# When the passes over the ada weights are issued among the weight loads of the first phase: a table of due counts in place of one rate per load

## The chip, the cores and the metric

One core of one Trainium2 chip runs the kernel, in float32 throughout. The time is that of one execution on the device, in microseconds (us): the median of three runs. A profiled execution is a run of its own; its span is what the trace covers.

## The reference, cut to what matters

One layer over 256 tokens of width 2048. A vector `c` conditions it: `mod` is a matrix-vector product with a weight of 2048 x 12288, cut into six vectors, and the first two (shift and scale) go into the first activation `h`, which the projections read.

```python
c_act = jax.nn.silu(c)
mod = (c_act @ w_ada[l] + b_ada[l])[:, None, :]
sh1, sc1, g1, sh2, sc2, g2 = jnp.split(mod, 6, axis=-1)
h = rmsnorm(x, ng[0]) * (1.0 + sc1) + sh1
proj = h @ w_in[l]
...
x = x + g1 * rmsnorm(mixed @ w_out[l], ng[1])
h = rmsnorm(x, ng[2]) * (1.0 + sc2) + sh2
f = jnp.square(jax.nn.relu(h @ w_ff1[l])) @ w_ff2[l]
x = x + g2 * rmsnorm(f, ng[3])
```

## The kernel before

**Products.** Every float32 weight is split into a high part and a remainder, and a product takes three matmuls (`natural_block`, L197 to L203): high by high, high activation by low weight, low activation by high weight. So a weight tile costs a cast on ACT (`h_v`, L152), a subtraction on DVE (`l_v`, L153) and three matmuls for each half of the tokens.

**The first phase** (L436 to L460) computes the columns `v_a`, `v_b`, `r_a` of `proj`: 12 result tiles (`nat`) of 512 columns. The 16 slices of `h` (128 features each, `hT`, two to a tile) come in four steps of 2, 4, 5 and 5 (`STEPS`). In a step, each slice's load brings the weights of the first four result tiles for that slice; then twice as many loads bring those of the other eight, which need all slices of the step. A load is one transfer of 1 MB (`r_v`) that feeds 24 matmuls, and there are 48, numbered 0 to 47: the slices 0 and 1 are loads 0 and 1, the slices 2 to 5 are loads 6 to 9, 6 to 10 are loads 18 to 22, 11 to 15 are loads 33 to 37. At the end of a step each result tile is evicted from PSUM: copied by ACT in the first step (`COPY`, L409), added by DVE in the others (`TENSOR_TENSOR`, L411).

**Rows of h.** Slice `k` of `h` needs the shift and the scale for its 128 features. Each is one pass (`ada_step`, L288): a transfer of 1 MB (`ad_0_k` or `ad_1_k`) and one DVE instruction of 2048 columns (L296) that multiplies by `c` and sums. There are 32 passes for the 16 slices, numbered here 1 to 32 in the order `ad_0_0`, `ad_1_0`, `ad_0_1`, and so on; all but the first two go through a pool of two buffers, so a pass's transfer is issued only when the pass two before it is done. `h_tile` (L353) then makes the slice: ACT adds the bias to the shift (L355) after the first pass, forms the scale (L356) after the second, writes the high part (L366) and the full value (L367); DVE multiplies by the norm (L363, for up to four slices at once) and subtracts for the low part (L368).

**Who sets the order.** `chunk` (L415) is called once per load. `ada_until` (L397) issues passes until a count is reached, then the load and its split are issued, then `h_ready` (L402) makes each slice whose passes have been issued. The count is the larger of what the slice at hand needs and of a rate (0.86 a load, L27 and L424). A scheduler places the instructions on each engine's queue, and each queue is executed in the order so made; all these transfers are issued by SP, in its order.

```python
ada_until(min(2 * KT, max(2 * need, 2 + int(ADA_RATE * at))))
```

Of the kernel before, what the change touches and what calls it, by code (L numbers as in the profile page):

```python
# [17 lines left out]
KT = D // P  # L18
# [5 lines left out]
FB = 8  # L24
EPS = 1e-6
NEG = -1.0e30
ADA_RATE = 0.86  # L27
APART = ("ss", "se", "ew")

SLOTS = 24  # L30
STEPS = (2, 4, 5, 5)
QUAD = 4
# [4 lines left out]
def trunk_kernel(ctx, tc, xT, xn, cT, ada, bcol, ngcol, w_alow, w_gup, gg_row,  # L37
# [118 lines left out]
    def wsplit(src, name, n=2048, step=2048):  # L156

        raw = load(src, f"r_{name}", n, step)
        return [split_one(raw, name, u, min(1024, n - 1024 * u)) for u in range((n + 1023) // 1024)]
# [179 lines left out]
    nat = vA + vB + rA  # L339
    with tc.tile_pool(name="st", bufs=1) as st:  # L340
# [53 lines left out]

        ready = [2, 0]

        def ada_until(n):  # L397
            while ready[0] < n:
                made["ada"] = next(steps)
                ready[0] += 1  # L400

        def h_ready():  # L402
            while ready[1] < KT and 2 * (ready[1] + 1) <= ready[0]:
                h_tile(ready[1])
                ready[1] += 1
# [9 lines left out]
        def chunk(need):  # L415
            nonlocal at
            with ExitStack() as order:
                order.enter_context(tc.issue_after(late.ins))
                if at < 2:
                    order.enter_context(tc.high_priority())  # L420
                    h_ready()
                    order.enter_context(tc.issue_after((lows or placed)[-1].ins))
                    order.enter_context(tc.issue_after(made["dve"].ins))
                ada_until(min(2 * KT, max(2 * need, 2 + int(ADA_RATE * at))))  # L424
                if at < 2:
                    h_ready()
            with ExitStack() as order:
                order.enter_context(tc.issue_after(placed[0].ins))
                if at < 2:
                    order.enter_context(tc.issue_after(made["act"].ins if at else late.ins))  # L430
                parts = wsplit(w_nat[at], f"v_{at}", step=2048 if at else 1024)
            h_ready()
            at += 1
            return parts

        for g, size in enumerate(STEPS):  # L436
            pv = [awake if g + n == 0 else pp(f"pv_{g}_{n}") for n in range(QUAD)]
            for k in range(size):
                parts = chunk(k0 + k + 1)
                for n in range(QUAD):  # L440
                    for i in range(NTOK):
                        natural_block(pv[n][:, i], hT[k0 + k], block(parts, n, 512), i, k == 0, k == size - 1)
                    if k == size - 1:
                        evict(nat[n], pv[n], g)
                if g + k == 0:

                    for _ in range(AWAKE):
                        pe.matmul(pv[0][:, 0, 0:384], negm[:, P:2 * P], carry, start=False, stop=False)
            todo = [(n, k) for n in range(QUAD, len(nat)) for k in range(size)]
            for j, (n, k) in enumerate(todo):  # L450
                if j % 4 == 0:
                    parts = chunk(k0 + size)
                if k == 0:
                    pv = pp(f"pv_{g}_{n}")
                for i in range(NTOK):
                    natural_block(pv[:, i], hT[k0 + k], block(parts, j % 4, 512), i, k == 0, k == size - 1)
                if k == size - 1:
                    evict(nat[n], pv, g)
            k0 += size
# [9 lines left out]
    if True:  # L469
# [8 lines left out]
        for u in range(2):  # L478
# [5 lines left out]
            for k in range(8):  # L484
                kt = 8 * u + k
# [573 lines left out]
```

## Time and profile before

| | before |
|---|---|
| median of 3 runs (lowest, highest) | 1798.25 us (1797.36, 1798.36) |
| the profiled execution, its span | 1800.57 us, 1798.6 us |
| PE busy, share of the span | 1772.9 us, 99% |
| DVE busy | 1283.8 us, 71% |
| ACT busy | 889.0 us, 49% |
| HBM | 428.18 MB read, 239 GB/s over the span |

The span lacks what lies around the program on the device, 1.97 us in that execution. An engine's busy time is the union of its instructions; matmuls overlap in the records (each is shown for 0.39 us where they start every 0.23 us), so a PE that is busy is not one that loses nothing. The first phase lies between 23 and 297 us of the span.

### The profile page before, as it was taken

What the parts mean: (1) busy time and instruction counts of PE and PEld (TensorE: products, weight loads), DVE (VectorE), ACT (ScalarE), POOL (GpSimd) and SP (SyncE); (2) the same over time, 40 slices, a digit from 0 to 9 for tenths busy, and PEclk for the clock granted to TensorE, in tenths of its full rate; (3) what the DMA queues carried; (4) which work ended last, traced back from release to release, by engine and by line L of the source; (5) the groups of instructions that cost most, each with busy time, mean ns of one, the idle gap of its engine ahead of it and who ended that gap; (6) DMA issues with size and microseconds to landing.
All of it is one profiled execution on the core that took longest, in us unless ns stands there. A gap on an engine that the chain in (4) does not pass through costs nothing.

```text
span 1798.6 us, 21945 instructions
## 1 busy us (share of the span) xinstructions
PE 1772.9 (99%) x8627; PEld 1471.8 (82%) x8627; DVE 1283.8 (71%) x1486; ACT 889.0 (49%) x1214; POOL 15.9 (1%) x34
## 2 busy tenths in 40 slices
PE   7999999999999999999999999999999999999997
PEld 4787887877888888888888878888888888888886
DVE  7899976887777788887786567565656565656566
ACT  6644444655553455555644455443434343434443
POOL 0000000000000000000000000000000000000000
PEclk9999999999999999999999999999999999999999
DMA  9888865666788776767777653555555555555552
GB/s 352 336 314 331 357 238 194 259 224 234 294 319 300 285 295 251 266 257 269 292 305 271 245 209 141 192 186 201 186 194 188 187 187 189 187 196 185 202 186 98
DMA packets 62313, 431.72 MB, mean 240 GB/s; under 512 B 7345, under 2 KB 7521, under 8 KB 11138
## 3 DMA queue, kind: packets, MB, share of 16 engines
q1 hardware_dynamic: 60000, 425.78, 63.6%
q10 hardware_dynamic: 2210, 4.54, 0.8%
q8 instruction: 67, 1.10, 0.2%
q14 instruction: 36, 0.29, 0.0%
HBM read 428.18 MB, written 2.12 MB: 239 GB/s over the span
## 4 chain that ended last, share of the span: by engine, by line
PE 92%; DVE 4%; issue 1%; ACT 1%; DMA 1%; POOL 0%; SPq 0%; POOLq 0%; DVEq 0%; ACTq 0%
PE pb_f L174 19%; PE pa_f L202 6%; PE pa_f L201 6%; PE pa_f L200 6%; PE pb_kb L174 5%; PE pb_qb L174 5%; PE pv L201 4%; PE pv L200 4%; PE pv L202 4%; PE pb_qa L174 3%; PE pb_ka L174 2%; DVE ad L296 2%; PE pa_yb L200 2%; PE pa_yb L201 2%; PE pa_wo L202 2%; PE pa_wo L200 2%
## 5 line engine op out<-in xcount | busy, mean ns | idle before, releaser
L153 DVE TENSOR_TENSOR l_f<-r_f,h_f 128x1024 fp32r<-128x1024 f32 x248 | 303.7, 1225 | 202.2 <-ACT h_f L152 198.5
L152 ACT CAST h_f<-r_f 128x1024 fp32r<-128x1024 f32 x248 | 261.0, 1053 | 262.9 <-PE pa_f L202 196.4
L174 PE MATMUL pb_f<-h,h_f 128*128 128x512 f32 x960 | 336.1, 399 | 0.0
L174 PE MATMUL pb_f<-h,l_f 128*128 128x256 f32 x960 | 259.8, 281 | 0.0
L296 DVE SCALAR_TENSOR_TENSOR ad<-ad,cb 128x2048 f32<-128x2048 f32 x96 | 219.1, 2286 | 20.0 <-DMA ad<-in_ada_dram 17.2
L174 PEld LDWEIGHTS pb_f<-h,h_f 128*128 128x128 f32 x960 | 177.0, 188 | 39.1
L200 PE MATMUL pa_f<-h_f,ft 128*128 128x512 f32 x512 | 199.3, 389 | 0.0
L202 PE MATMUL pa_f<-h_f,ft 128*128 128x512 f32 x512 | 199.2, 389 | 0.0
L201 PE MATMUL pa_f<-l_f,ft 128*128 128x512 f32 x512 | 199.2, 389 | 0.0
L174 PEld LDWEIGHTS pb_f<-h,l_f 128*128 128x128 f32 x960 | 181.3, 189 | 5.8
L200 PE MATMUL pv<-h_v,hT 128*128 128x512 f32 x384 | 148.6, 394 | 6.8 <-ACT hT L366 3.6
L201 PE MATMUL pv<-l_v,hT 128*128 128x512 f32 x384 | 149.6, 393 | 0.5 <-DVE l_v L153 0.5
L202 PE MATMUL pv<-h_v,hT 128*128 128x512 f32 x384 | 147.7, 389 | 0.0
L153 DVE TENSOR_TENSOR l_v<-r_v,h_v 128x1024 fp32r<-128x1024 f32 x96 | 114.5, 1219 | 31.2 <-ACT h_v L152 31.0
L152 ACT CAST h_v<-r_v 128x1024 fp32r<-128x1024 f32 x96 | 97.8, 1048 | 56.0 <-PE pv L202 48.5
L201 PEld LDWEIGHTS pa_f<-l_f,ft 128*128 128x128 f32 x512 | 96.1, 188 | 20.1
L202 PEld LDWEIGHTS pa_f<-h_f,ft 128*128 128x128 f32 x512 | 96.1, 188 | 19.9
L200 PEld LDWEIGHTS pa_f<-h_f,ft 128*128 128x128 f32 x512 | 96.1, 188 | 19.7
L200 PEld LDWEIGHTS pv<-h_v,hT 128*128 128x128 f32 x384 | 71.7, 188 | 25.8 <-ACT h_v L152 6.6
L174 PE MATMUL pb_qb<-hT,h_qb 128*128 128x512 f32 x256 | 92.1, 400 | 0.0
L174 PE MATMUL pb_kb<-hT,h_kb 128*128 128x512 f32 x256 | 90.7, 393 | 0.0
L201 PEld LDWEIGHTS pv<-l_v,hT 128*128 128x128 f32 x384 | 72.4, 189 | 17.3 <-DVE l_v L153 2.2
(284 smaller groups left out, 3286.5 us busy)
## 6 DMA issues: line engine op xcount, KB each, us to landing
r_f<-in_w_f_dram SPq DMA_DIRECT2D x124, 1024.0 KB, 4.8
ad<-in_ada_dram SPq DMA_DIRECT2D x96, 1024.0 KB, 5.5
r_v<-in_w_nat_dram SPq DMA_DIRECT2D x47, 1024.0 KB, 7.3
r_ga<-in_w_ga_dram SPq DMA_DIRECT2D x16, 1024.0 KB, 4.9
r_ya<-in_w_ao_dram SPq DMA_DIRECT2D x16, 1024.0 KB, 5.7
r_qb<-in_w_qb_dram SPq DMA_DIRECT2D x16, 1024.0 KB, 5.6
r_kb<-in_w_kb_dram SPq DMA_DIRECT2D x16, 1024.0 KB, 4.8
r_gb<-in_w_gb_dram SPq DMA_DIRECT2D x16, 1024.0 KB, 4.9
```

The source lines that it names most:

```text
L152: s_.copy(hi[:, 0:m], raw)
L153: lows.append(v_.tensor_tensor(out=lo[:, 0:m], in0=raw, in1=hi[:, 0:m].bitcast(F32), op=ALU.subtract))
L174: pe.matmul(o, l, r, start=kt == 0 and n == 0, stop=kt == KT - 1 and n == 1)
L200: pe.matmul(ps, ah, w[0], start=start, stop=False)
L201: pe.matmul(ps, ah, w[1], start=False, stop=False)
L202: return pe.matmul(ps, al, w[0], start=False, stop=stop)
L296: return v_.scalar_tensor_tensor(out=raw, in0=raw, scalar=1.0, in1=cb, op0=ALU.mult, op1=ALU.mult, accum_out=mods[:, m, kt:kt + 1])
```

## The change

The rate goes. A table `due` gives, for the loads 2 to 36, how many passes are to have been issued by that load. It is anchored at one load ahead of the last slice of each step but the first (loads 8, 21 and 36, with 12, 22 and 32 passes) and runs evenly from one anchor to the next, starting with 4 passes at load 1. What a slice needs at its own load still holds as a minimum.

```diff
-ADA_RATE = 0.86
...
         ready = [2, 0]
 
+        due, a0, n0, o, kt = {}, 1, 4, 0, 0
+        for size in STEPS:
+            kt += size
+            o += size
+            if o > 2:
+                for a in range(a0 + 1, o - 1):
+                    due[a] = n0 + (2 * kt - n0) * (a - a0) // (o - 2 - a0)
+                a0, n0 = o - 2, 2 * kt
+            o += size * (len(nat) - QUAD) // 4
+
         def ada_until(n):
...
-                ada_until(min(2 * KT, max(2 * need, 2 + int(ADA_RATE * at))))
+                ada_until(min(2 * KT, max(2 * need, due.get(at, 0))))
```

Passes issued by the time a load is issued:

| load | 1 | 2 | 3 | 4 | 5 | 6 | 7 | 8 | 9 | 10 | 12 | 14 | 17 | 20 | 21 | 22 | 24 | 32 | 35 | 36 |
|---|---|---|---|---|---|---|---|---|---|---|---|---|---|---|---|---|---|---|---|---|
| before | 4 | 4 | 4 | 5 | 6 | 7 | 8 | 10 | 12 | 12 | 12 | 14 | 16 | 19 | 20 | 22 | 22 | 29 | 32 | 32 |
| change | 4 | 5 | 6 | 7 | 8 | 9 | 10 | 12 | 12 | 13 | 15 | 16 | 18 | 21 | 22 | 22 | 24 | 29 | 31 | 32 |

No instruction is added or taken away. Below, `ad_m_k` is the pass of vector m (0 shift, 1 scale) for slice k, `r_v_n` the raw weights of load n, `h_v_n_u` and `l_v_n_u` the two parts of its half u, `sh1` and `A1` shift and scale, `xs` the value before the split, `pv_g_n` the sum of result tile n in step g; a number at a name's end is the buffer's. The change's line numbers in `h_tile` and the split are one lower, those of evictions nine higher.

**SP, loads 2 to 4.** Before:

```order
L140 DMA r_v_2_304<-in_w_nat_dram 128x2048
L140 DMA r_v_3_342<-in_w_nat_dram 128x2048
L295 DMA ad_0_2_380<-in_ada_dram 128x2048
L140 DMA r_v_4_383<-in_w_nat_dram 128x2048
L295 DMA ad_1_2_421<-in_ada_dram 128x2048
L140 DMA r_v_5_424<-in_w_nat_dram 128x2048
```

Now:

```order
L139 DMA r_v_2_307<-in_w_nat_dram 128x2048
L294 DMA ad_0_2_304<-in_ada_dram 128x2048
L294 DMA ad_1_2_345<-in_ada_dram 128x2048
L139 DMA r_v_3_348<-in_w_nat_dram 128x2048
L294 DMA ad_0_3_393<-in_ada_dram 128x2048
L139 DMA r_v_4_396<-in_w_nat_dram 128x2048
```

Both passes of slice 2 now stand ahead of load 3, which stood ahead of them.

**DVE, from the first half of load 2.** Before:

```order
L153 TENSOR_TENSOR l_v_2_0_307<-r_v_2_304,h_v_2_0_306 128x1024
L153 TENSOR_TENSOR l_v_2_1_311<-r_v_2_304,h_v_2_1_310 128x1024
L153 TENSOR_TENSOR l_v_3_0_345<-r_v_3_342,h_v_3_0_344 128x1024
L296 SCALAR_TENSOR_TENSOR ad_0_2_380,mods_144<-ad_0_2_380,cb_128 128x2048
L153 TENSOR_TENSOR l_v_3_1_349<-r_v_3_342,h_v_3_1_348 128x1024
L153 TENSOR_TENSOR l_v_4_0_386<-r_v_4_383,h_v_4_0_385 128x1024
L153 TENSOR_TENSOR l_v_4_1_390<-r_v_4_383,h_v_4_1_389 128x1024
L296 SCALAR_TENSOR_TENSOR ad_1_2_421,mods_144<-ad_1_2_421,cb_128 128x2048
L363 TENSOR_TENSOR xs0_83<-xs0_83,rs_186 128x512
```

Now:

```order
L152 TENSOR_TENSOR l_v_2_0_310<-r_v_2_307,h_v_2_0_309 128x1024
L295 SCALAR_TENSOR_TENSOR ad_0_2_304,mods_144<-ad_0_2_304,cb_128 128x2048
L152 TENSOR_TENSOR l_v_2_1_314<-r_v_2_307,h_v_2_1_313 128x1024
L295 SCALAR_TENSOR_TENSOR ad_1_2_345,mods_144<-ad_1_2_345,cb_128 128x2048
L362 TENSOR_TENSOR xs0_83<-xs0_83,rs_186 128x512
L152 TENSOR_TENSOR l_v_3_0_351<-r_v_3_348,h_v_3_0_350 128x1024
L152 TENSOR_TENSOR l_v_3_1_355<-r_v_3_348,h_v_3_1_354 128x1024
L295 SCALAR_TENSOR_TENSOR ad_0_3_393,mods_144<-ad_0_3_393,cb_128 128x2048
L367 TENSOR_TENSOR hT1_361<-xs0_83,hT1_361 128x256
```

Passes 5 and 6 (`ad_0_2`, `ad_1_2`) stood behind load 3's first half and behind load 4's split; now both stand ahead of load 3's split, and pass 7 (`ad_0_3`) ahead of load 4's.

**ACT, around load 8.** Before:

```order
L152 CAST h_v_8_0_560<-r_v_8_558 128x1024
L152 CAST h_v_8_1_564<-r_v_8_558 128x1024
L366 ACTIVATE hT2_571<-xs1_85,sh1_164,A1_165 128x256
L367 ACTIVATE xs1_85<-xs1_85,sh1_164,A1_165 128x256
L355 ACTIVATE sh1_164<-mods_144,bc_sb_91 128x1
L356 ACTIVATE A1_165<-mods_144,b1g_166,ng_sb_93 128x1
L366 ACTIVATE hT2_571<-xs1_85,sh1_164,A1_165 128x256
L152 CAST h_v_9_0_607<-r_v_9_605 128x1024
```

Now:

```order
L151 CAST h_v_7_1_530<-r_v_7_524 128x1024
L365 ACTIVATE hT2_537<-xs1_85,sh1_164,A1_165 128x256
L366 ACTIVATE xs1_85<-xs1_85,sh1_164,A1_165 128x256
L354 ACTIVATE sh1_164<-mods_144,bc_sb_91 128x1
L355 ACTIVATE A1_165<-mods_144,b1g_166,ng_sb_93 128x1
L365 ACTIVATE hT2_537<-xs1_85,sh1_164,A1_165 128x256
L151 CAST h_v_8_0_573<-r_v_8_571 128x1024
L151 CAST h_v_8_1_577<-r_v_8_571 128x1024
```

The casts of load 8 stood ahead of the shift and scale of slice 5 (`sh1` and `A1` in the pieces, which wait for passes 11 and 12); now they stand behind them and behind that slice's high part, and the casts of load 9 follow load 8's with only that slice's `xs1` between.

**DVE, from load 10.** Before:

```order
L153 TENSOR_TENSOR l_v_10_0_651<-r_v_10_648,h_v_10_0_650 128x1024
L411 TENSOR_TENSOR vA0_149<-pv_1_0_469,vA0_149 128x1024
L411 TENSOR_TENSOR vA1_150<-pv_1_1_470,vA1_150 128x1024
L411 TENSOR_TENSOR vA2_151<-pv_1_2_471,vA2_151 128x1024
L411 TENSOR_TENSOR vA3_152<-pv_1_3_472,vA3_152 128x1024
L153 TENSOR_TENSOR l_v_10_1_655<-r_v_10_648,h_v_10_1_654 128x1024
L153 TENSOR_TENSOR l_v_11_0_687<-r_v_11_684,h_v_11_0_686 128x1024
L153 TENSOR_TENSOR l_v_11_1_691<-r_v_11_684,h_v_11_1_690 128x1024
L153 TENSOR_TENSOR l_v_12_0_723<-r_v_12_720,h_v_12_0_722 128x1024
```

Now:

```order
L152 TENSOR_TENSOR l_v_10_0_654<-r_v_10_651,h_v_10_0_653 128x1024
L420 TENSOR_TENSOR vA2_151<-pv_1_2_482,vA2_151 128x1024
L420 TENSOR_TENSOR vA3_152<-pv_1_3_483,vA3_152 128x1024
L152 TENSOR_TENSOR l_v_10_1_658<-r_v_10_651,h_v_10_1_657 128x1024
L295 SCALAR_TENSOR_TENSOR ad_1_6_687,mods_144<-ad_1_6_687,cb_128 128x2048
L152 TENSOR_TENSOR l_v_11_0_693<-r_v_11_690,h_v_11_0_692 128x1024
L420 TENSOR_TENSOR vB0_153<-pv_1_4_661,vB0_153 128x1024
L152 TENSOR_TENSOR l_v_11_1_697<-r_v_11_690,h_v_11_1_696 128x1024
L367 TENSOR_TENSOR hT3_702<-xs1_85,hT3_702 128x256
```

Pass 14 (`ad_1_6`) has come in ahead of load 11's split, and the eviction `vB0` between that load's halves. Pass 13, which stood behind load 12, and the evictions `vA0` and `vA1` are just ahead of the piece now.

## Rows read from the trace of the kernel before

**Rows 1.** The page, its part on the chain of work that ended last: shares of the span by engine.
```profile
PE 92%; DVE 4%; issue 1%; ACT 1%; DMA 1%; POOL 0%; SPq 0%; POOLq 0%; DVEq 0%; ACTq 0%
```

**Rows 2.** Busy time of each engine in four stretches of 20 us, three with stalls and one without. The columns: the stretch, its length, busy us of PE, PEld, DVE, ACT and POOL with the number of instructions, the granted clock, the share of the DMA engines that was busy, GB/s.
```profile
60.00:80.00 20.00, 17.18 (x75) 13.53 (x73) 15.64 (x16) 9.72 (x15) 0.00 (x0) 1.00 0.83 331
80.00:100.00 20.00, 19.77 (x79) 15.75 (x80) 18.58 (x17) 11.03 (x13) 0.00 (x0) 0.91 0.89 351
140.00:160.00 20.00, 19.05 (x82) 14.83 (x81) 16.30 (x17) 10.94 (x15) 0.00 (x0) 1.00 0.91 372
240.00:260.00 20.00, 20.00 (x90) 16.57 (x89) 14.65 (x14) 8.12 (x8) 0.00 (x0) 1.00 0.53 195
```

**Rows 3.** PE in order of time, the end of the first step and the slices of the second. Columns here and in rows 4, 6, 7 and 8: start, us, engine, line, operation, result and inputs with shapes, how many in a row; in brackets the idle time before and what ended it.
```profile
57.64 0.39 PE L200 MATMUL pv<-h_v,hT 128*128 128x512 f32 x1
...
71.01 0.39 PE L202 MATMUL pv<-h_v,hT 128*128 128x512 f32 x1
72.53 0.50 PE L200 MATMUL pv<-h_v,hT 128*128 128x512 f32 x1 [1.13 <-ACT hT L366]
...
77.93 0.39 PE L202 MATMUL pv<-h_v,hT 128*128 128x512 f32 x1
80.23 2.17 PE L200 MATMUL pv<-h_v,hT 128*128 128x512 f32 x4 [1.92 <-ACT h_v L152]
82.19 1.86 PE L201 MATMUL pv<-l_v,hT 128*128 128x512 f32 x4
83.89 0.39 PE L202 MATMUL pv<-h_v,hT 128*128 128x512 f32 x1
```

**Rows 4.** PE in order of time, the last slice of the third step.
```profile
152.63 0.39 PE L202 MATMUL pv<-h_v,hT 128*128 128x512 f32 x1
153.50 0.73 PE L200 MATMUL pv<-h_v,hT 128*128 128x512 f32 x2 [0.48 <-ACT h_v L152]
...
156.47 0.40 PE L202 MATMUL pv<-h_v,hT 128*128 128x512 f32 x1
```

**Rows 5.** PE in stretches of 2 us: length, busy us, granted clock, share of the DMA engines, GB/s. The first two lie around the gap before the first slice, the others are the restart after the gap before the last slice of the second step.
```profile
20.00:22.00 2.00, 0.50 (x2) 1.00 1.01 422
22.00:24.00 2.00, 1.03 (x3) 1.00 1.01 422
80.00:82.00 2.00, 1.77 (x4) 0.61 1.08 451
82.00:84.00 2.00, 2.00 (x6) 0.53 0.95 397
```

**Rows 6.** DVE in order of time. L296 is an ada pass, L153 the second half of a split, L363 and L368 are parts of a row of h, L411 is an eviction.
```profile
32.51 4.63 DVE L153 TENSOR_TENSOR l_v<-r_v,h_v 128x1024 fp32r<-128x1024 f32 x4 [0.51 <-ACT h_v L152]
...
38.54 2.28 DVE L296 SCALAR_TENSOR_TENSOR ad<-ad,cb 128x2048 f32<-128x2048 f32 x1
...
48.00 0.08 DVE L296 DVE_READ_ACCUMULATOR ad<-ad,cb 128x1 f32 x1
...
69.59 0.08 DVE L296 DVE_READ_ACCUMULATOR ad<-ad,cb 128x1 f32 x1
...
78.11 0.08 DVE L296 DVE_READ_ACCUMULATOR ad<-ad,cb 128x1 f32 x1
80.21 2.36 DVE L153 TENSOR_TENSOR l_v<-r_v,h_v 128x1024 fp32r<-128x1024 f32 x2 [2.02 <-ACT h_v L152]
...
85.01 4.62 DVE L411 TENSOR_TENSOR vA<-pv,vA 128x1024 f32<-128x1024 f32 x4 [0.97 <-PE pv L202]
89.55 4.62 DVE L153 TENSOR_TENSOR l_v<-r_v,h_v 128x1024 fp32r<-128x1024 f32 x4
...
96.36 2.28 DVE L296 SCALAR_TENSOR_TENSOR ad<-ad,cb 128x2048 f32<-128x2048 f32 x1
```

**Rows 7.** ACT in order of time. L152 is a cast (the first half of a split), L409 an eviction of the first step, L355, L356, L366 and L367 make a row of h.
```profile
31.45 3.88 ACT L152 CAST h_v<-r_v 128x1024 fp32r<-128x1024 f32 x4
...
41.52 1.02 ACT L409 COPY vB<-pv 128x1024 f32<-128x1024 f32 x1 [0.28 <-PE pv L202]
42.43 1.99 ACT L152 CAST h_v<-r_v 128x1024 fp32r<-128x1024 f32 x2
...
76.01 0.30 ACT L355 ACTIVATE sh<-mods,bc_sb 128x1 f32<-128x1 f32 x1 [2.89 <-DVE ad L296]
78.22 0.39 ACT L356 ACTIVATE A<-mods,b1g,ng_sb 128x1 f32<-128x1 f32 x1 [1.92 <-DVE ad L296]
78.64 0.60 ACT L366 ACTIVATE hT<-xs,sh,A 128x256 fp32r<-128x256 f32 x1
79.15 1.97 ACT L152 CAST h_v<-r_v 128x1024 fp32r<-128x1024 f32 x2
```

**Rows 8.** SP's DMA issues in order of time. Of the three in the first row the third is load 3's.
```profile
14.98 5.49 SPq L140 DMA_DIRECT2D r_v<-in_w_nat_dram  x3
27.67 0.33 SPq L295 DMA_DIRECT2D ad<-in_ada_dram  x1
```

**Rows 9.** DVE by line and form between 60 and 235 us: busy us, mean ns of one, idle time before it and what ended it.
```profile
L153 DVE TENSOR_TENSOR l_v<-r_v,h_v 128x1024 fp32r<-128x1024 f32 x64 | 75.9, 1218 | 10.9 <-ACT h_v L152 10.9
L296 DVE SCALAR_TENSOR_TENSOR ad<-ad,cb 128x2048 f32<-128x2048 f32 x24 | 54.6, 2283 | 0.0
```

**Rows 10.** DMA issues by line between 67 and 68 us, where one pass is fetched with nothing else in flight: count, KB each, median us from issue to landing.
```profile
ad<-in_ada_dram SPq DMA_DIRECT2D x1, 1024.0 KB, 4.8
```

## The prediction

> **What bounds the kernel now.** I read four views: the chain that ended last, the engines' busy time by stretch, PE in order of time where PE is idle, and the queues of DVE, ACT and SP beside it. The chain is 92% PE [rows 1], so what PE loses in the first phase is lost at the end, and what it does not lose there cannot be won. By stretch, PE is full from 240 to 260 us and has gaps in 60 to 100 and 140 to 160 us [rows 2]. A phase matmul starts every 0.227 us: the 59 starts from 57.64 to 71.01 us take 13.37 us [rows 3]. What PE loses I take as the time from one start to a later one, less 0.227 us for each start between.
>
> Three places lose something. **Slice 4** starts at 72.53 instead of 71.24 us: 1.3 us, released by that slice's row of h on ACT. **Slice 5**: from 77.93 to 83.89 us nine starts take 5.96 instead of 2.04 us, 3.9 lost [rows 3]. About 2.07 of it is the wait that ends at 80.23 us with the cast of load 9; the rest is the clock, which was granted at 0.61 and 0.53 in the next 4 us [rows 5], so that eight matmuls took 3.66 instead of 1.81 us: PE came out of the wait at the lower of its two levels, 1.2 GHz, and lost 1.85 us more by it. **Slice 10**: nine starts from 152.63 to 156.47 us take 3.84 instead of 2.04 us, 1.8 lost [rows 4]. Together 7.0 us; this is all that the change can win.
>
> Why slice 5 is late is seen on ACT: shift and scale of that slice wait for passes 11 and 12, which end just before 76.01 and at 78.19 us, then come its high part and only then the casts of load 9 at 79.15 us [rows 6, 7]. ACT takes its queue in order, so a cast whose data are there stands behind a scale that waits for a pass.
>
> **The change, part by part.** Nothing is added or removed; most passes go one to four loads earlier on SP, DVE and ACT, passes 31 and 32 one later. I walk the new order with the trace's durations: an instruction starts when the one ahead of it on its engine has let go and when what it waits for is done. The end of a record overlaps the next by some 0.08 us, which I take off. On DVE a half split holds the engine 1.14 us (4.63 for four), a pass 2.21, the multiplications of 512 and 1024 columns 0.6 and 1.14, an eviction 1.14 [rows 6]; on ACT a cast holds it 0.95 (3.88 for four), an eviction 0.91, the rows of h 0.2, 0.3, 0.5 and 0.5 [rows 7]. A transfer lands 4.8 us after its issue [rows 10], or 2.5 us after the one ahead when they queue (1 MB at 422 GB/s [rows 5]). Up to load 2 nothing differs.
>
> *Loads 3 to 5.* SP now issues load 3 behind passes 5 and 6, which wait for buffers that come free at 27.67 us and one pass later, 29.9, so at 30.3 instead of by 20.5 us [rows 8]; it lands at 37.6, which costs nothing, since its casts come later still. DVE does pass 5 at 35.9 (32.51 and three half splits), the second half of load 2, pass 6 at 39.3 and `xs` until 42.1. On ACT load 3's casts stand behind the eviction that PE releases at 41.52 [rows 7]; they run at 42.4 and 43.4, and PE, which reaches load 3 at 44.0 (71.24 less five loads of 24 x 0.227 us), waits 0.2. Pass 7 then runs from 45.8 to 48.0; the shift waits for it, and load 4's casts behind the shift run at 48.5 and 49.5. PE is there at 49.7 and loses 0.65. Pass 8 ends at 54.1; behind scale and high part the first cast of load 5 runs at 55.3, PE is there at 55.8: 0.6. The half's remainder ends at 57.6: 1.0 more. Pass 9 stands between the halves of load 5; the second remainder ends at 61.0, PE wanted it at 60.4: 0.65. Sum **3.1 us**, where nothing was lost before. Bounds: nothing, as in these loads before, and 6.6 if passes 7, 8 and 9 all fell on PE; the walk has it near the middle.
>
> *Slices 2 to 5.* PE reaches load 6 at 63.5 (44.0 + 3 x 5.44 + 3.1), finds loads 6 and 7 all but ready, and wants load 8 at 74.5. DVE ends load 6's split at 64.8, pass 10 at 67.0, `xs` at 68.2, load 7's split at 70.8, pass 11 at 73.3 and pass 12 at 75.6. ACT's scale of slice 5 waits for pass 12, its high part ends at 76.6, and load 8's first cast, now behind it, at 77.6. (Load 8's transfer, issued on SP behind pass 12's at 67.6, lands at 74.4, ahead of that.) PE loses **3.1 us** at slice 4 in place of 1.3 there and 2.07 at slice 5. The wait is longer than the one after which the clock fell; I take the same **1.85 us** for the clock. Slice 5 itself finds all ready. Sum of the two places 5.0 (with 0.07 at load 7), where 5.2 was lost.
>
> *Loads 10 to 16.* Before, no pass stands between 78.2 and 96.36 us, and DVE does splits and evictions alone [rows 6]. Now passes 13 and 14 lie among them (4.4 us), and remainders of loads 10, 11, 12 and 16 come late: the same walk gives waits of 0.3, 0.6, 0.55 and 0.3. Sum **1.8 us**. Bounds: nothing, as before, and 4.4 if both passes fell on PE. I keep near the lower end, since DVE comes to this stretch with load 9's split done early.
>
> *Slice 10 and loads 23, 24.* The passes of slice 10 are now due a load earlier, so the casts of load 22 are ahead of PE: of the 1.8 lost, 0.45 remains (at load 21's second half). Passes 23 and 24, which came with loads 25 and 26, come among loads 23 and 24: 0.75 where nothing was lost. The passes from 29 on move by no more than a load; after 250 us nothing differs.
>
> Sum: now 3.1 + 5.0 + 1.8 + 0.45 + 0.75 = 11.1 us lost; before 1.3 + 3.9 + 1.8 = 7.0. The difference is **+4.1 us**. The sum is made within the profiled execution (1800.57 us, span 1798.6); the median is 2.3 us below that execution, and I carry the difference over: 1798.25 + 4.1 = **1802.3 us**. The same walk along the order of before gives 1.3 and 2.2 us at slices 4 and 5, where the trace has 1.3 and 2.07; I allow half a microsecond of error at a place.
>
> One rule speaks for the change. The row says that DVE never stood idle ahead of a pass (24 passes between 60 and 235 us, 0.0 us idle) and 10.9 us ahead of remainders, for casts on ACT [rows 9]: transfers of passes were always early enough. The Trainium skill, in "DMA: Bandwidth & Descriptors", section "Rules for kernel authors", advises to issue a transfer early, compute meanwhile, and wait late. By that rule alone fetching the passes earlier would bring the 7.0 us and 1791.2; the trace shows no wait of that kind to win, and what the earlier passes do is to hold the queues that splits share.
>
> **The rivals.**
> *The change does what it says (faster).* If the passes fill gaps of DVE that nobody wants, all three stalls go: 1798.25 - 7.0 = 1791.2. For it: slices 4 and 5 wait for passes, and DVE has gaps, 2.02 us ahead of 80.21 alone [rows 6]. Against it: those gaps are casts that are late on ACT, and ACT's casts get the passes ahead of them. It decides by whether load 8's first cast starts before 74.5 us; in my walk it misses by 2 us, and pass 12 can't start before its transfer has a buffer, when pass 10 is done. Chance 0.05, with a half-way gain in it.
> *The clock holds.* A gap of some 2.5 us before the first slice (1.50 and 0.97 us idle in the two stretches) left it at 1.00 [rows 5], one of 1.92 us did not [rows 3]. If it holds through the new stall, 1.85 goes: 1798.25 + 2.25 = 1800.5. The new wait is longer than both: 0.2.
> *The clock falls once more.* Loads 4 and 5 lose 0.6, 0.6 and 1.0 us within 7 us. A fall there costs up to 1.85: 1804.2. A gap of this size, 1.13 us ahead of 72.53, had no such effect [rows 2, 3]: 0.12.
> *The waits are half as long as walked,* because casts and remainders overlap better: 1.5 to 3 us above before, say 1800.6. 0.13.
>
> **How the numbers follow.** My forecast (3.2 to 4.8 us slower) has 0.5. About 0.2%, 3.6 us, is what a measurement here can tell from no change; the forecast lies just beyond it, with 0.38 of its chance beyond and 0.12 within. Slower: 0.38 + 0.12 = 0.5. Same: 0.12 + 0.2 + 0.13, and 0.01 of the first rival, 0.46. Faster: 0.04. The range goes from 1799.6 (the clock holds and the waits are somewhat shorter, +1.4) to 1804.6 (the clock falls twice, and 0.5 of error).
>
> **What would show it.** Right: PE gaps at about 50, 56, 57.5 and 60 us that before does not have; no gap ahead of slice 5; one of about 3 us ahead of slice 4, ended by the cast of load 8, with the clock near 0.5 behind it; the wait at 153 us mostly gone; small gaps ended by `l_v` between 92 and 102 us. Wrong: slice 4 starts before 76 us of the span, or PE runs through loads 4 and 5; then the casts did not stand behind the passes as the order has it, and the kernel is faster.

## The result, and the profile after

The changed kernel takes **1804.24 us** (median of 9 runs, 1801.19 to 1805.59) beside 1798.41 us for the kernel before (9 runs, 1797.36 to 1799.65): ratio 1.0028, 95% interval [1.002, 1.0037], 3.6 to 6.7 us slower. Forecast were 1802.3 us, between 1799.6 and 1804.6; the time lies 0.4 us below the upper end. The profiled execution is the run of 1804.24 us, its span 1802.2 us.

The page still puts the chain that ended last on PE, so what the first phase loses is still lost at the end [rows 1]:

```profile
PE 92%; DVE 4%; ACT 2%; issue 1%; DMA 1%; POOL 0%; SPq 0%; POOLq 0%; DVEq 0%; ACTq 0%
```

Two stretches of PE in order of time, with the columns of [rows 3]: the places that had no idle time before, and slices 4 and 5.

```profile
48.04 0.40 PE L199 MATMUL pv<-h_v,hT 128*128 128x512 f32 x1
48.88 0.49 PE L199 MATMUL pv<-h_v,hT 128*128 128x512 f32 x1 [0.45 <-ACT h_v L151]
49.22 0.48 PE L200 MATMUL pv<-l_v,hT 128*128 128x512 f32 x1
49.53 0.40 PE L201 MATMUL pv<-h_v,hT 128*128 128x512 f32 x1
...
54.08 0.39 PE L201 MATMUL pv<-h_v,hT 128*128 128x512 f32 x1
54.93 0.50 PE L199 MATMUL pv<-h_v,hT 128*128 128x512 f32 x1 [0.47 <-ACT h_v L151]
56.19 0.50 PE L200 MATMUL pv<-l_v,hT 128*128 128x512 f32 x1 [0.76 <-DVE l_v L152]
...
58.86 0.39 PE L199 MATMUL pv<-h_v,hT 128*128 128x512 f32 x1
59.54 0.50 PE L200 MATMUL pv<-l_v,hT 128*128 128x512 f32 x1 [0.29 <-DVE l_v L152]
```

```profile
73.15 0.39 PE L201 MATMUL pv<-h_v,hT 128*128 128x512 f32 x1
76.37 2.17 PE L199 MATMUL pv<-h_v,hT 128*128 128x512 f32 x4 [2.83 <-ACT h_v L151]
78.33 0.63 PE L200 MATMUL pv<-l_v,hT 128*128 128x512 f32 x1
...
82.58 0.39 PE L200 MATMUL pv<-l_v,hT 128*128 128x512 f32 x1
...
84.89 0.39 PE L199 MATMUL pv<-h_v,hT 128*128 128x512 f32 x1
```

Gaps end near 49, 55, 56 and 59.5 us, and there is the long one ahead of slice 4. The forecast had them near 50, 56, 57.5 and 60, on the time scale of the execution before, whose first phase began 1.92 us later. Slice 5 (the last row, from 84.89 us) loses nothing. A record lasts 0.39 us where starts are 0.227 us apart, so a wait is read from start to start: 3.22 us from 73.15 to 76.37, less 0.227, is 2.99 us waited. The wait of 1.92 us ahead of slice 5 and the one at slice 10 [rows 3, 4] have gone.

What stood ahead of load 8's casts, on DVE (the two passes of slice 5, and load 8's remainders behind them), on ACT (shift, scale and high part of slice 5, then the casts), and on SP the issues around load 8, with the landing of load 8 in a row of its own (count, KB, us to landing):

```profile
69.82 2.29 DVE L295 SCALAR_TENSOR_TENSOR ad<-ad,cb 128x2048 f32<-128x2048 f32 x1
...
72.03 2.29 DVE L295 SCALAR_TENSOR_TENSOR ad<-ad,cb 128x2048 f32<-128x2048 f32 x1
...
76.35 2.36 DVE L152 TENSOR_TENSOR l_v<-r_v,h_v 128x1024 fp32r<-128x1024 f32 x2 [2.02 <-ACT h_v L151]
```

```profile
72.15 0.30 ACT L354 ACTIVATE sh<-mods,bc_sb 128x1 f32<-128x1 f32 x1 [2.89 <-DVE ad L295]
74.36 0.39 ACT L355 ACTIVATE A<-mods,b1g,ng_sb 128x1 f32<-128x1 f32 x1 [1.92 <-DVE ad L295]
74.78 0.60 ACT L365 ACTIVATE hT<-xs,sh,A 128x256 fp32r<-128x256 f32 x1
75.29 1.97 ACT L151 CAST h_v<-r_v 128x1024 fp32r<-128x1024 f32 x2
```

```profile
58.37 7.79 SPq L294 DMA_DIRECT2D ad<-in_ada_dram  x2
66.25 0.86 SPq L139 DMA_DIRECT2D r_v<-in_w_nat_dram  x2
```

```profile
r_v<-in_w_nat_dram SPq DMA_DIRECT2D x1, 1024.0 KB, 7.9
```

The first row of SP is passes 11 and 12: behind the issue of pass 11 SP was held until pass 12 had a buffer, at 65.8 us, and load 8 is the first of the two loads behind them. Load 8 landed at 66.25 + 7.9 = 74.2 us; its first cast started at 75.29, behind the scale that waited 1.92 us for pass 12 and the high part. The clock behind that wait, in stretches of 2 us (columns of [rows 5], all engines):

```profile
74.00:76.00 2.00, 0.00 (x0) 0.00 (x0) 0.33 (x2) 1.61 (x3) 0.00 (x0) 0.93 1.07 442
76.00:78.00 2.00, 1.63 (x4) 1.09 (x5) 1.65 (x2) 2.00 (x4) 0.00 (x0) 0.50 0.96 406
78.00:80.00 2.00, 2.00 (x6) 1.56 (x5) 2.00 (x3) 1.65 (x2) 0.00 (x0) 0.50 1.07 451
80.00:82.00 2.00, 2.00 (x6) 1.57 (x5) 2.00 (x3) 0.00 (x0) 0.00 (x0) 0.50 0.94 397
82.00:84.00 2.00, 2.00 (x9) 1.57 (x9) 1.52 (x2) 0.44 (x2) 0.00 (x0) 0.87 1.06 442
```

PE ran at its lower level, 1.2 GHz, for three stretches and a little of a fourth, where before it was not two [rows 5].

Counted load by load (24 starts each, less 5.44 us, which is 24 starts without a loss), from load 3 on:

| lost, us | loads 3 to 6 | load 7, up to slice 4 | load 8 | load 9 | 10 to 16 | 21 | 22 | 23, 24 | 35 | sum |
|---|---|---|---|---|---|---|---|---|---|---|
| before | 0 | 1.29 | 2.26 | 1.89 | 0.01 | 0.64 | 1.17 | 0.25 | 0.25 | 7.76 |
| after | 3.96 | 3.04 | 3.08 | 0 | 2.03 | 0.38 | 0 | 0.87 | 0 | 13.36 |

That is 5.6 us more. The first phase's first matmul came 1.92 us earlier in this profiled execution than in that of before, so that its last matmul came 3.74 us later, and the span is 3.6 us longer.

### The profile page after: what moved, and what is told of

Read it like the earlier page. It is cut to its first block, busy times and chain, and to the rows that moved or that the text cites. A ratio compares the mean times of both kernels' runs of the same rounds, so it can differ in the third digit from the quotient of the medians.

```text
span 1802.2 us, 21944 instructions
## 1 busy us (share of the span) xinstructions
PE 1775.5 (99%) x8627; PEld 1472.6 (82%) x8627; DVE 1284.1 (71%) x1486; ACT 887.4 (49%) x1214; POOL 15.9 (1%) x34
## 4 chain that ended last, share of the span: by engine, by line
PE 92%; DVE 4%; ACT 2%; issue 1%; DMA 1%; POOL 0%; SPq 0%; POOLq 0%; DVEq 0%; ACTq 0%
PE pb_f L173 19%; PE pa_f L200 6%; PE pa_f L199 6%; PE pa_f L201 6%; PE pb_kb L173 5%; PE pb_qb L173 5%; PE pv L200 4%; PE pv L201 4%; PE pv L199 3%; PE pb_qa L173 3%; PE pb_ka L173 2%; DVE ad L295 2%; PE pa_gb L200 2%; PE pa_yb L199 2%; PE pa_wo L199 2%; PE pa_yb L200 2%
## 5 line engine op out<-in xcount | busy, mean ns | idle before, releaser
L152 DVE TENSOR_TENSOR l_f<-r_f,h_f 128x1024 fp32r<-128x1024 f32 x248 | 303.8, 1225 | 202.5 <-ACT h_f L151 198.8
L199 PE MATMUL pv<-h_v,hT 128*128 128x512 f32 x384 | 150.9, 399 | 6.5 <-ACT h_v L151 3.7
L201 PE MATMUL pv<-h_v,hT 128*128 128x512 f32 x384 | 150.0, 392 | 0.0
L152 DVE TENSOR_TENSOR l_v<-r_v,h_v 128x1024 fp32r<-128x1024 f32 x96 | 114.6, 1220 | 34.2 <-ACT h_v L151 34.1
```

Of the source, the lines that this page charges most:

```text
L152: lows.append(v_.tensor_tensor(out=lo[:, 0:m], in0=raw, in1=hi[:, 0:m].bitcast(F32), op=ALU.subtract))
L199: pe.matmul(ps, ah, w[0], start=start, stop=False)
L201: return pe.matmul(ps, al, w[0], start=False, stop=stop)
```

## The experiments

Each time is a median, the ratio is to the kernel before on the same chip with its 95% interval. "Phase" is the time from the start of the first matmul of the first phase to that of its last, in the profiled execution; it leaves out the start, which varies. That execution is one run of several: in e_early, e_p12, e_pool and e_fixed_pool it is the lowest of them, in e_fill_a the highest.

| | us | ratio | phase, us |
|---|---|---|---|
| before | 1798.41 | | 273.43 |
| after | 1804.24 | 1.0028 [1.002, 1.0037] | 279.09 |
| e_early | 1801.45 | 1.0013 [1.0004, 1.0022] | 274.48 |
| e_late | 1801.97 | 1.0021 [1.0012, 1.003] | 276.92 |
| e_casts | 1801.86 | 1.0015 [1.0006, 1.0024] | 275.36 |
| e_fill_a | 1802.75 | 1.0018 [1.0009, 1.0026] | 276.56 |
| e_fill_b | 1798.19 | 0.9994 [0.9985, 1.0003] | 273.22 |
| e_p12 | 1802.07 | 1.0018 [1.0008, 1.0027] | 276.22 |
| e_pool | 1802.87 | 1.0023 [1.0014, 1.0033] | 270.69 |
| e_pool5 | 1795.91 | 0.9982 [0.9973, 0.9991] | 270.00 |
| e_fixed_pool | 1799.36 | 1.0001 [0.9992, 1.001] | 272.38 |
| e_due_pool | 1798.31 | 0.9997 [0.9988, 1.0006] | 274.26 |
| e_best | 1794.57 | 0.9976 [0.9965, 0.9986] | 268.74 |

The kernel before had medians of 1798.41 to 1799.58 us in the four series. In the expectations, "T" is the prediction's theory: a loss is made where casts on ACT and remainders on DVE stand behind passes and rows of h.

### One half of the table at a time

**e_early**: new due times for loads 0 to 9 alone.

```diff
+ADA_RATE = 0.86
...
-ada_until(min(2 * KT, max(2 * need, due.get(at, 0))))
+ada_until(min(2 * KT, max(2 * need, due.get(at, 0) if at < 10 else 2 + int(ADA_RATE * at))))
```

> The new due times for loads 0 to 9 alone, the fixed rate of 0.86 from load 10 on. Theory (T): every loss is made where it shows, by casts on ACT and remainders on DVE that stand behind passes and rows, so the first half carries the loss: loads 3 to 6 cost 3.96 us and loads 7 and 8 cost 6.12 us in the changed kernel, against 5.44 us in loads 7 to 9 before, and slice 10 keeps the 1.8 us of before: +4.6 us, 1803.0 us; PE idle some 2.8 us ahead of slice 4, 0.6 to 1.0 us at loads 4 and 5, a wait near 155 us as before. Rival (S): the start of the program, which differs between the two profiled executions by 1.9 us, or the later loads carry it: then this kernel is within 2 us of the kernel before, 1798.4 to 1800.4.

Loads 3 to 6 lost 3.88 us and load 7 3.03 us, as in the changed kernel, and slice 10's stall was half back (0.74 and 0.25 us). But load 8 lost 0.63 instead of 3.08 us: behind the same wait (2.83 us idle in both) the clock held.

```profile
74.00:76.00 2.00, 0.00 (x0) 0.00 (x0) 0.30 (x2) 1.63 (x3) 0.00 (x0) 1.00 1.06 446
76.00:78.00 2.00, 1.44 (x5) 0.92 (x6) 1.68 (x2) 2.00 (x4) 0.00 (x0) 1.00 0.97 406
78.00:80.00 2.00, 2.00 (x11) 1.63 (x10) 2.00 (x3) 2.00 (x3) 0.00 (x0) 1.00 1.08 414
```

PE does nothing from 74 to 76 us in both kernels, and is granted 0.50 after it in one execution and 1.00 in the other. So the waits are where T has them, and what the clock takes differs from one execution to another. The ratio (1.0013, 2.3 us) lies between what T and what its rival expected; the waits decide for T, the size does not.

**e_late**: the other half, `due.get(at, 0) if at > 9 else 2 + int(ADA_RATE * at)`.

> The fixed rate of 0.86 for loads 0 to 9, the new due times from load 10 on. Losses that only add up load by load would give what the changed kernel's later loads cost against before, 2.03 + 1.25 us against 2.31 us: +1.0 us, 1799.4 us, with slices 4 and 5 as before. Theory (T), followed along this order: passes 13 and 14 are due from load 10 on, but pass 12 has only just been fetched at load 9, so pass 13's row stands ahead of load 10's casts on ACT and pass 14 (fetched only when a buffer comes free) ahead of load 11's remainders on DVE: one wait of 3 to 4 us near 88 us ended by a remainder, which the load-by-load sum does not have, then a lower clock behind it, and no wait at slice 10: +2.5 us without the clock, up to +5 with it: 1801 to 1803.5 us.

1801.97 us, as T expected: the order decides, not a sum by load. Load 10 alone lost 4.80 us, in a wait of 2.88 us ended by a remainder (first row, PE) and the lower clock behind it; loads 11 to 22 lost nothing.

```profile
90.57 0.58 PE L201 MATMUL pv<-l_v,hT 128*128 128x512 f32 x1 [2.88 <-DVE l_v L153]
```

```profile
88.00:90.00 2.00, 0.00 (x0) 0.00 (x0) 2.00 (x3) 1.79 (x2) 0.00 (x0) 1.00 1.05 434
90.00:92.00 2.00, 1.43 (x4) 1.16 (x5) 2.00 (x3) 0.00 (x0) 0.00 (x0) 0.71 0.98 410
92.00:94.00 2.00, 2.00 (x7) 1.54 (x6) 2.00 (x3) 0.10 (x1) 0.00 (x0) 0.50 1.03 426
```

**e_p12**: the kernel before with its rule for one pass changed.

```diff
-ada_until(min(2 * KT, max(2 * need, 2 + int(ADA_RATE * at))))
+ada_until(min(2 * KT, max(2 * need, 12 if at == 8 else 2 + int(ADA_RATE * at))))
```

> The kernel before with one due time changed: pass 12 at load 8 instead of load 9, which is the changed kernel's rule (a step's last pass one load ahead of its last slice) by itself. If the pass alone were what slice 5 waits for, its 3.9 us would go: 1795.2 us. Theory (T), following the order: passes 11 and 12 stand in line behind passes 9 and 10 for two buffers, their transfers can't start before 66.7 and 68.9 us, load 8's casts stand on ACT behind slice 4's scale and load 9's transfer on SP behind that of pass 12, so slice 4 stays late by 1 to 1.3 us, slice 5 waits for passes 11 and 12 one behind the other and for load 9's casts behind both, 6 to 8.5 us in one wait with the clock low behind it, and slice 10 has nothing left to wait for (minus 2 us): 2.5 to 5 us more than before, 1801.7 to 1804 us.

1802.07 us. One wait of 8.47 us, and slice 5 and slice 10 lose nothing. It stands ahead of slice 4, not of slice 5: on ACT the high parts of both slices came behind slice 5's scale, and on DVE the multiplication by the norm that slice 4's high part needs came behind pass 12 (PE, ACT, DVE).

```profile
77.71 0.80 PE L200 MATMUL pv<-h_v,hT 128*128 128x512 f32 x1 [8.47 <-ACT hT L366]
```

```profile
73.51 0.29 ACT L355 ACTIVATE sh<-mods,bc_sb 128x1 f32<-128x1 f32 x1 [3.69 <-DVE ad L296]
75.83 0.39 ACT L356 ACTIVATE A<-mods,b1g,ng_sb 128x1 f32<-128x1 f32 x1 [2.03 <-DVE ad L296]
76.12 1.03 ACT L152 CAST h_v<-r_v 128x1024 fp32r<-128x1024 f32 x1
77.06 1.09 ACT L366 ACTIVATE hT<-xs,sh,A 128x256 fp32r<-128x256 f32 x2
```

```profile
75.71 1.22 DVE L363 TENSOR_TENSOR xs<-xs,rs 128x1024 f32<-128x1024 f32 x1
```

That multiplication is placed behind the last pass issued (`made["ada"]` in `h_tile`). With 12 passes due at load 8, where the rate had 8 at load 7, slices 4 and 5 are made together behind pass 12; in the changed kernel slice 4 is made at load 7, behind pass 10. So the change's rule for the last pass of a step, by itself, costs about as much as the whole change (1.0018 and 1.0028, the intervals overlap), but partly by a path that the changed kernel does not have. Here too an ACT instruction that waited for a late pass (3.69 us) held what the order had put behind it.

### The clock

**e_fill_a**: the changed kernel with matmuls that add zeros ahead of slice 4.

```diff
                 parts = chunk(k0 + k + 1)
+                if k0 + k == 4:
+                    for _ in range(4):
+                        pe.matmul(pv[0][:, 0, 0:384], negm[:, P:2 * P], carry, start=False, stop=False)
```

> The changed kernel with four extra matmuls of 128x384 (zeros added into an accumulator, the same that the kernel issues behind its first slice, some 0.685 us each) on PE ahead of slice 4, so that 2.74 of the 2.83 us that PE waits there are filled; nothing else moves. Clock theory: the wait itself stays (PE's first useful matmul of slice 4 at the same time behind the load before it), but the clock stays at 1.00, and load 8's 24 matmuls lose 0 to 0.6 instead of 3.08 us. In the run of the new due times for loads 0 to 9 alone the same wait of 3.03 us was followed by the full clock, so in part of the executions nothing is to be won: 1.5 to 3 us less than the changed kernel, 1801.3 to 1802.8 us, and a smaller spread than its 4.4 us. Rival: the fall has other causes than that idle time (the phase of the clock against it): same median and spread as the changed kernel, 1804 us.

Load 7 lost the same 3.02 us, load 8 0.62; the clock stayed at 1.00:

```profile
76.00:78.00 2.00, 1.90 (x6) 0.76 (x4) 0.11 (x2) 1.82 (x3) 0.00 (x0) 1.00 0.96 401
78.00:80.00 2.00, 1.64 (x6) 1.07 (x7) 1.87 (x2) 2.00 (x4) 0.00 (x0) 1.00 1.06 446
```

The runs lay between 1801.03 and 1803.36 us, 2.3 us apart where the changed kernel's lay 4.4 apart. The median is 1.5 us lower, by the ratios, which take out the difference between the series, 1.8 us, and the ratios' intervals overlap. In the profiled executions the clock is worth 3.08 - 0.62 = 2.46 us; how much it is on average over executions is not settled. This execution's first phase began at 22.90 us, as late as in that of before, and loads 3 to 6 lost 3.94 us, as in the changed kernel's, which began at 21.03: the waits do not come from the start.

**e_fill_b**: the same with `k0 + k == 5` and three matmuls, in the kernel before.

> The kernel before with three of these extra matmuls (2.05 us) ahead of slice 5, where PE waits 1.92 us for the cast of load 9 and the clock fell afterwards. Clock theory: load 9 loses 0.2 or less instead of 1.89 us in executions where it fell: 0.9 to 1.9 us less than before, 1797.2 to 1798.2 us. Rival: no change within 0.5 us. In either case nothing else of the profile moves.

The clock held at 1.00 there too, but loads 8 and 9 lost 2.74 + 1.16 instead of 2.26 + 1.89 us: 0.25 less, not 1.9. Load 8 lost 0.48 more because pass 12's transfer landed late (DVE idle 0.40 us ahead of that pass): issued at the same time after the phase's first matmul as in before (46.8 us), it took 6.7 instead of 5.1 us, which the edit does not explain. Load 9 lost only 0.73 less: at full clock PE had to wait for its second cast and its remainder (0.22 and 0.24 us idle), which the slow restart had covered. 1798.19 us lies at the upper end of what was expected, and the ratio is not told from 1. More than half of what the slow clock cost there was hidden by work that was late anyway.

### Which queue makes the casts late

**e_casts**: in the changed kernel, a row's ACT instructions are, from load 2 on, placed behind the casts of the load they are recorded with.

```diff
-    loads, lows = [], []
+    loads, lows, casts = [], [], []
...
-        s_.copy(hi[:, 0:m], raw)
+        casts.append(s_.copy(hi[:, 0:m], raw))
...
-            h_ready()
+            with ExitStack() as order:
+                if at >= 2:
+                    order.enter_context(tc.issue_after(casts[-1].ins))
+                h_ready()
```

> The changed kernel, but from load 2 on the ACT instructions of a slice's row (shift, scale, high part, x) are placed behind the last cast of the load they are recorded with; the passes keep their due times. Theory (T): the casts stood behind shift and scale, so loads 4 and 5 fall from 1.45 and 1.79 us to some 0.45 each, load 6 to 0.2, and slice 4's wait from 2.83 us to 1.5 + 0.8 us: that rest is load 8's transfer, which stands on SP behind that of pass 12 and lands only then. 3 to 4 us less than the changed kernel: 1800.4 us if the clock falls at slice 4 as it does there, 1797.3 us if it holds. Rival (D): DVE's own queue makes the loss (passes ahead of remainders), and the order on ACT is nothing: 1804 us, the same waits at the same places, ended by remainders instead of casts.

Half right. Loads 4, 5 and 6 lost 0.64 + 0.68 + 0.44 = 1.76 instead of 3.52 us, and the ratio fell from 1.0028 to 1.0015, with intervals that overlap. Slice 4 still waited 2.85 instead of 2.99 us (start to start), now for the transfer: ACT stood idle for 6.35 us until load 8 landed (ACT, then SP).

```profile
68.09 0.60 ACT L366 ACTIVATE xs<-xs,sh,A 128x256 f32<-128x256 f32 x1
75.05 1.99 ACT L151 CAST h_v<-r_v 128x1024 fp32r<-128x1024 f32 x2 [6.35 <-DMA r_v<-in_w_nat_dram]
```

```profile
66.25 0.33 SPq L294 DMA_DIRECT2D ad<-in_ada_dram  x1
66.67 0.86 SPq L139 DMA_DIRECT2D r_v<-in_w_nat_dram  x2
```

Load 8 is issued at 66.67, right behind pass 12, and takes 8.4 us. So at slice 4 two queues are late by nearly the same time (in the changed kernel the load lands at 74.2, the cast starts at 75.29): ACT, whose scale waits for pass 12, and SP, whose issue of pass 12 waits for the buffer that pass 10 frees. Taking one away leaves the other.

**e_pool**: the changed kernel with the transfers of passes 3 to 32 on a queue of their own, POOL's.

```diff
-                dma.dma_start(raw, ada[m, kt])
+                g_.dma_start(raw, ada[m, kt])
```

> The changed kernel with the transfers of passes 3 to 32 issued on POOL's queue instead of SP's, so that a load no longer stands behind a pass that waits for its buffer; due times as in the changed kernel. Rival (SP): it is SP's order that makes loads and their casts late, and what stands on ACT and DVE only follows from it: no wait at loads 3 to 6, slice 4 within 0.7 us, two small waits of 0.3 to 0.7 us in all: 9 to 12 us less than the changed kernel with the clock, 1792 to 1795 us. Theory (T), that the order on ACT and DVE is the cause whatever queue fetches the passes: the waits of loads 4, 5 and slice 4 stay, 1802 to 1804 us. If issuing on POOL costs DVE something (both would be slowed side by side), it shows as longer DVE records in loads 3 to 36.

No loss at loads 3 to 7, as the rival had it and T did not. But the first phase began at 27.18 us, since the inputs of the first slice came late beside loads and passes (the median of the four transfers of x was 10.7 us to landing, 5.3 in the changed kernel), and load 8 lost 5.02 us: its remainders stood on DVE behind pass 12, whose transfer, issued at 66.70, took 8.7 us. Phase 270.69 us, 8.4 less than the changed kernel; the time, 1802.87 us, lies where T expected it, by the late start and load 8 and not by T's waits.

**e_pool5**: passes 5 to 32 on POOL's queue, and pass 12 at load 9.

```diff
-                dma.dma_start(raw, ada[m, kt])
+                (g_ if kt > 1 else dma).dma_start(raw, ada[m, kt])
...
-ada_until(min(2 * KT, max(2 * need, due.get(at, 0))))
+ada_until(min(2 * KT, max(2 * need, {**due, **{8: 11, 9: 12}}.get(at, 0))))
```

> The changed kernel with the transfers of passes 5 to 32 on POOL's queue (1 to 4 stay on SP, since with all of them on POOL the inputs of the first slice came 5 us later) and pass 12 due at load 9 instead of 8, since with POOL's queue its transfer took 8.8 us beside the loads and load 8's remainders waited behind it. If SP's order was the cause of the late casts: first phase matmul at 21 to 23 us, no loss at loads 3 to 6 and slice 4, at most 1.0 us (and the clock, 1.9) at slice 5, nothing at slice 10: 3.7 to 6.7 us less than before, 1792.4 to 1795.4 us. If it was the 5 us of head start that the late first slice gave the loads: loads 4, 5 and slice 4 lose as in the changed kernel, 1800 to 1803 us.

1795.91 us, faster than both kernels. The phase begins at 20.77 us and loads 3 to 8 lose nothing, so it was not the head start. Left are 1.47 us at load 2 (its remainders stand behind pass 5, which waits for its transfer) and 2.86 us at load 9 (slice 5's low part on DVE behind pass 13).

**e_fixed_pool** and **e_due_pool**: the kernel before and the changed kernel, each with the first edit of e_pool5 alone.

> The kernel before (fixed rate 0.86) with the transfers of passes 5 to 32 on POOL's queue: the fourth corner beside before, the changed kernel and the new due times with POOL's queue. Theory (Q): SP's order, in which a load stands behind a pass that waits for a buffer, makes the casts late; the due times decide how late the slices' rows are. With the late due times the rows still come late whatever the queue: about 1.3 us at slice 4, 0.6 to 2.2 at slice 5, up to 3.5 at slice 10, and a pass whose transfer runs beside the loads' may hold remainders up to 5 us near load 10: no gain, 1799 to 1805 us. Rival: the queue is the whole of the gain and the due times don't matter: 1794 to 1797 us, as with the new due times.

> The changed kernel, all its due times as they are, with the transfers of passes 5 to 32 on POOL's queue. Theory (Q): as with pass 12 due at load 9 up to load 7 (no loss at loads 3 to 6 nor at slice 4, 1.5 us at load 2, where remainders stand behind pass 5), then load 8's remainders stand behind pass 12 as in the run with all passes on POOL's queue: 3.1 us there, and up to 1.9 us for the clock: 1.5 to 3.4 us less than before, 1796.2 to 1798.1 us. Rival: the passes' number on DVE makes the loss, whatever the queue: as the changed kernel, 1803 to 1805 us.

| ratio to before | passes on SP's queue | passes 5 to 32 on POOL's |
|---|---|---|
| fixed rate | 1 | 1.0001 [0.9992, 1.001] |
| new due times | 1.0028 [1.002, 1.0037] | 0.9997 [0.9988, 1.0006] |

The new due times cost 5 us with SP's queue and nothing that can be measured with POOL's: the loss as it was needs the passes on SP's queue. With POOL's, though, "nothing" is a balance. In e_due_pool loads 2, 3, 4, 6 and 7 lose nothing, but load 5 lost 1.19 us, which was not expected (its first remainder stood behind a pass that waited 3.43 us for its transfer), and load 8 lost 7.39 us, not 3.1 to 5, because pass 12 held its remainders (DVE) and the lower clock followed for three stretches. POOL's queue alone is worth nothing with the late due times: loads 6 and 22, the slices 2 and 10, lose 4.16 and 2.44 us, where rows of h come late; slices 4 and 5, where losses were expected too, lose nothing.

```profile
73.32 2.29 DVE L295 SCALAR_TENSOR_TENSOR ad<-ad,cb 128x2048 f32<-128x2048 f32 x1 [2.78 <-DMA ad<-in_ada_dram]
...
75.54 2.36 DVE L152 TENSOR_TENSOR l_v<-r_v,h_v 128x1024 fp32r<-128x1024 f32 x2
```

**e_best**: e_pool5 with the table mended at the two places that still lost time.

```diff
-ada_until(min(2 * KT, max(2 * need, due.get(at, 0))))
+ada_until(min(2 * KT, max(2 * need, {**due, **{2: 4, 3: 6, 8: 11, 9: 12, 10: 12, 11: 13}}.get(at, 0))))
```

> The changed kernel with the transfers of passes 5 to 32 on POOL's queue and the due times of the two places that still lost time there moved: pass 5 due at load 3 instead of 2 (load 2's remainders stood behind it, 1.5 us), pass 12 at load 9 instead of 8, pass 13 at load 11 instead of 10 (slice 5's low part stood on DVE behind pass 13's, 2.6 us). Theory (Q): no loss left at loads 2 to 9, at most 0.7 us near load 10 and none at slice 10; first phase matmul at 21 us: 265.8 to 266.7 us from the first phase matmul to the last, against 273.4 before, so 5 to 7.6 us less than before, 1791.5 to 1794 us. Rival: another wait comes in place of each one removed (the transfers share the same engines): 1796 us, as with the other due times on POOL's queue.

1794.57 us, 4.3 us below before, a little short of the expected range. Load 2 loses nothing; loads 8, 9 and 12 lose 0.37, 1.60 and 1.11 us, so part of what was removed did come back as other waits. PE's waits after 20 us:

```profile
PE pv L199 <- ACT hT L365: 2.2, 1, 2.2
PE pv L201 <- DVE hT L367: 1.1, 1, 1.1
PE pv L200 <- DVE l_v L152: 0.8, 1, 0.8
```

The first is the start of the phase; behind it two waits are left.

## Why the prediction was right

**Loads 3 to 5, forecast 3.1, lost 3.96 with load 6: the waits are right, a term is missing.** Start to start, less 0.227, the five waits are 0.21, 0.61, 0.62, 1.03 and 0.45 us, where the prediction had 0.2, 0.65, 0.6, 1.0 and 0.65. Of the other microsecond some 0.7 is the restart: behind each wait the next one or two starts come 0.31 to 0.34 us apart (48.88, 49.22, 49.53) instead of 0.227, 0.1 to 0.2 us a time. This was left out everywhere. The rest is a short wait at load 6 (0.13 us) and starts that come 0.23 us apart.

**Slice 4, forecast 3.1 of wait and 1.85 of clock: measured 2.99 and 2.46.** The wait is ended by load 8's cast, slice 5 is ready. The clock term was taken from one execution with a shorter wait; here the lower level lasted twice as long. "The clock holds" had a chance of 0.2, as if it were one case for the kernel: e_early shows it as something that differs by execution behind the same wait. That a median holds a mixture of the two follows from it, and in what shares is not known.

**Loads 10 to 16, forecast 1.8, lost 2.03; load 21 0.45 against 0.38; loads 23 and 24 0.75 against 0.87.** All in place, and slice 10's stall has gone.

**The sum, forecast 4.1, measured 5.6** in the profiled executions. The forecast for after is short by 0.9 at loads 3 to 6, by 1.1 at slice 4 (0.6 of it clock) and by 0.3 later; before's own losses were 7.76 instead of 7.0, which takes 0.8 back. What was mis-sized is restart and clock, not a wait. By the ratio, over all runs, the difference is 5.0 us (3.6 to 6.7). That 1804.24 us still lies inside the range is in part luck: the terms that were too small come to 2.3 us, losses of before that had not been counted take back 0.8, and the range's upper end had been set with a second fall of the clock at loads 4 and 5, where one fall that lasted twice as long came instead.

**Where the reasoning was too narrow.** The prediction made ACT's order the whole cause at slice 4, since load 8's transfer was to land at 74.4 us, 3.2 us ahead of the cast. Counted from the phase's first matmul, as the two executions began 1.92 us apart, the cast was forecast at 54.7 us and came at 54.3, but the transfer was forecast at 51.5 us and landed at 53.2: it took 7.9 us from its issue, not 6.8. So the transfer was only 1.1 us ahead of the cast, and it would by itself have made most of the wait. e_casts shows the same: ACT's order makes half of loads 4 to 6, and with it taken away slice 4 waited 0.14 us less. e_due_pool shows that with the passes on POOL's queue loads 3, 4, 6 and 7 lose nothing. What moved the passes earlier also moved loads behind passes on SP, and that was walked for loads 3 and 8 alone, for load 8 with too short a transfer. In e_pool the orders of ACT and DVE differ too, presumably since the scheduler places them by when it expects the loads, and so they do in e_due_pool; so how much of loads 3 to 6 is SP's order directly, and how much the order of casts that follows from it, was not separated.

**The rivals.** That the change does what it says (1791.2 us) did not come; load 8's first cast started at 75.29 us, past the 74.5 that would have decided for it, in an execution that began 1.9 us earlier. The waits were not half as long as walked. A second fall of the clock at loads 4 and 5 was not seen. The Trainium skill, in "DMA: Bandwidth & Descriptors", section "Rules for kernel authors", advises to issue a transfer early and to wait for it late. That did pay here where the early transfers had a queue of their own and the passes did not stand ahead of remainders: 4.3 us in e_best, of the 7.0 that it would give by itself.

## What to carry to other kernels

Before work is issued earlier, write down for every queue that it enters what now stands behind it, the queue that issues transfers first of all: an early transfer that had to wait for a buffer held every transfer behind it (SP, some 7 us ahead of pass 12 in the changed kernel). Two queues can be late by the same amount at the same place; only taking them away one at a time, and then both, shows it. Price a wait with its restart and with a clock that falls in some executions, and count from start to start.

## What the runs showed of the hardware that was not expected

**The clock behind a wait is not a function of the wait alone.** Behind PE's idle time from about 73.5 to 76.3 us the grant was 0.50 for three stretches of 2 us in one execution and 1.00 throughout in another (above), and behind the shorter wait ahead of slice 5, before, it fell as well [rows 5]. The gap ahead of the phase's first matmul says the same. It was 2.51 or 2.52 us in six profiled executions; behind it, from 22 to 24 us, the grant was 0.50 in those of the changed kernel and e_early, and 1.00 in those of e_fill_b, e_p12, e_pool5 and e_fixed_pool. That such a gap leaves the clock up, which the prediction took from the kernel before, did not hold in the changed kernel; it cost nothing there, since load 0 took the same time in all.

**The start of the program has two lengths.** In 12 profiled executions with the same start the first phase matmul came at 20.8 to 21.3 us (6) or at 22.3 to 23.0 us (6). The difference is one group of four matmuls ahead of the first pass, which took 3.78 us in the profiled execution of before and 1.98 us in that of after:

```profile
6.50 3.78 PE L267 MATMUL sp_cb<-dg_cb,ones 128*128 128x512 f32 x4 [6.50 <-DVE dg_cb L264]
11.17 3.78 PE L267 MATMUL sp_cb<-dg_cb,ones 128*128 128x512 f32 x4 [0.89 <-ACT cb L268]
```

```profile
6.39 3.78 PE L266 MATMUL sp_cb<-dg_cb,ones 128*128 128x512 f32 x4 [6.39 <-DVE dg_cb L263]
11.04 1.98 PE L266 MATMUL sp_cb<-dg_cb,ones 128*128 128x512 f32 x4 [0.87 <-ACT cb L267]
```

The clock accounts for it. Each trace lists the grants from a first entry on, which is 1.00 in all, and the clock's column shows 1.00 ahead of it only because nothing is listed there. That entry stands at 9.6 to 10.9 us in the six early executions, ahead of the second group, and at 14.6 to 15.8 us in the six late ones, behind it; behind the first of a group, matmuls start 0.85 us apart ahead of that entry and 0.43 us apart behind it. Of the scatter of a kernel's runs, 1.8 us can come from this.

**A pass takes longer on POOL's queue beside the loads.** On SP's queue a pass landed 4.8 us after its issue when alone [rows 10]; on POOL's queue, with loads running beside it, one took 8.7 us. Between 20 and 100 us the median was 5.0 us for 11 passes on SP's queue in the kernel before, 6.4 us for 12 in the changed kernel, and 8.2 us for 13 passes on POOL's in e_best. No run has POOL's queue without loads beside it, so that it is the shared engines, and not the queue itself, is not shown.
